# Hybrid attention layer on one core: taking GpSimd out of the projections

## The chip, the cores and the metric

The kernel runs on one core of a Trainium2 chip. The metric is the device time of one execution in microseconds. What is quoted is the median of several runs.

## What is computed

The reference is one decoder layer on 512 tokens of width 1024, all in float32:

```python
h = rms_norm(x, attn_pre_norm)
proj = h @ w_in                 # dq dk dv | nq | kc vc ks vs kw vw | gates
dq, dk, nq, kc, ks, kw = (apply_rope(t, cos, sin) for t in ...)
o_diff = diff_attention(dq, dk, dv, lam)       # 4 heads, two softmax maps each
o_nsa  = nsa_attention(nq, kc, vc, ks, vs, kw, vw, gates, ...)   # 8 heads, 3 branches
x = x + rms_norm(concat(o_diff, o_nsa) @ w_out, attn_post_norm)
h = rms_norm(x, ffn_pre_norm)
x = x + rms_norm((silu(h @ w_gate) * (h @ w_up)) @ w_down, ffn_post_norm)
```

`apply_rope` takes the halves x1, x2 of a head and returns x1·cos − x2·sin and x1·sin + x2·cos. The `nsa` branch also compresses kc and vc through a small two-layer network (`w1`, `w2`).

## The kernel before

**Precision.** TensorE multiplies rounded values (float32r). Each operand is therefore split into a rounded high part and a low part that holds the rest, and a product is the sum of three: high by high, high by low, low by high. For a weight tile of 128x1024 this is `split_w` (lines 108 to 113): a rounding copy `whi` (line 104 on ScalarE, 106 on VectorE) and a subtraction `wlo` (line 112, on VectorE or GpSimd). Raw weights, high and low parts have three buffers each, so a DMA for a new weight tile waits until a low part three tiles earlier is done.

**Start.** `load_x` brings the eight 128x512 pieces of the transposed x, and makes `xh` (line 195, ScalarE), `xl` (196, VectorE) and, in place over the raw piece, its square (199, GpSimd). VectorE adds the squares (203); TensorE sums them over the partitions, and from that come `rstd` and the four tables cos, sin, ckv, skv, which carry the factor rstd (line 246, in which VectorE reads the factor from PSUM).

**Projections.** The list `ORDER` writes the order of the stages. `C` is the pair kc, vc; `q0 k0 q1 k1 n0 n1 s` are the seven other pairs of 128x512 tiles (the two halves of the rotated heads); `v0 v1` and `g` are the projections that need no rotation; `ck cv` are the two compressions. One tile of a pair is `fm_tile`: 24 matmuls of 512 columns into one PSUM bank. These banks have the tag `mm`, of which there are two; `v`, `g`, the compressions and the later `mixp` use the same tag, and a compression holds its bank until its last weight tile has come. After each tile ScalarE copies PSUM to SBUF with the scale (line 282), and four products with the tables follow: t1, t2 (283, 284) on VectorE, a·sin, b·cos (285, 286) and then the sum (293), the second low part (300) and the odd tile's weight low part (112) on `e2`. `e2` is GpSimd for six of the eight pairs and VectorE for the two in `FAST`. The rotated high and low parts go to DRAM, and the heads load them from there.

**Who rounds.** `HIF`, `HIT` and `HIQ` name the weights (of pairs 1 and 5, of g, v0 and v1) and the rotated values (of pairs 1, 6 and 7) whose rounding VectorE does in place of ScalarE. `alt` gives every second low part of v0, g and the compressions to GpSimd.

**Heads and the rest.** `D0` to `D3` and `N0` to `N7` are attention heads. They are built with a higher priority, so that they are interleaved with the later projections from about 125 us on. In them GpSimd multiplies rows of the softmax (`row_mul`, line 505). After them come the output projection, the norms and the feed-forward products; these last run from about 354 us to the end.

**Order on the engines.** A planner orders the instructions of every engine before the run, from the priorities, the data they need and its own costs; on the chip each engine takes its list in that order. All DMAs are issued by the queue of SP, in order too.

Of the kernel before, what the change touches and what calls it, by code (L numbers as in the profile page):

```python
# [12 lines left out]
AF = mybir.ActivationFunctionType  # L13
OP = mybir.AluOpType
# [26 lines left out]
NVG = 4 * HEAD_DIM + 3 * NSA_HEADS  # L41
DQ0, DK0, KCVC, DQ1, DK1, NQ0, KSKW, NQ1 = range(8)
# [5 lines left out]
    "D3 F0 F1 M3 N7"  # L48
)
HP = 400  # L50
FAST = (1, 3)
POOL_LO = "157"
PSB = {"mm": 2, "sc": 3, "tr": 2, "av": 1}
MIX_A = (0, 1, 4, 5)
# [9 lines left out]
HP2 = 1  # L64
NS = 36
WB = (3, 3, 3)
LOD = ("v1",)
HP3 = 60
PREE = "adad"
TRH = ("tr", "gu", "tr", "tr")  # L70
HIF = (1, 5)
HIT = ("g", "v0", "v1")
HIQ = (1, 6, 7)
OTH = "a"
OTL = "p"
HIS = "d"
# [4 lines left out]
def hybrid_block_kernel(  # L81
# [6 lines left out]
    act, dve, pool, pe = nc.scalar, nc.vector, nc.gpsimd, nc.tensor  # L88

    def f32(ap):  # L90
        return ap.bitcast(F32)
# [10 lines left out]
    def to_r(eng, dst, src):  # L102
        if eng == "a":
            act.activation(dst, src, AF.Copy)  # L104
        else:
            dve.tensor_copy(dst, src)

    def split_w(raw, w=1024, lo_eng=None, hi_eng="a"):
        hi = wpool.tile([P, 1024], F32R, tag="hi", name="whi", bufs=WB[1])
        lo = wpool.tile([P, 1024], F32R, tag="lo", name="wlo", bufs=WB[2])  # L110
        to_r(hi_eng, hi[:, :w], raw[:, :w])
        (lo_eng or dve).tensor_tensor(lo[:, :w], raw[:, :w], f32(hi[:, :w]), OP.subtract)  # L112
        return hi, lo
# [42 lines left out]
    def sslot(name, dt=F32R):  # L156
        return S.tile([P, SEQ], dt, tag="s", name=name)
# [6 lines left out]
    def ps(tag, name, dt=F32):  # L164
        return PS.tile([P, SEQ], dt, tag=tag, name=name, bufs=PSB[tag])
# [18 lines left out]
    def rope_tile():  # L184
        return R.tile([P, 4, SEQ], F32R, tag="rope", name="rope")
# [3 lines left out]
    def load_x(k):  # L189
        if k % 2 == 0:  # L190
            xraws[k // 2] = T.tile([P, 2, SEQ], F32R, tag="k", name="xraw", bufs=BUFS["k"])
        t = f32(xraws[k // 2][:, k % 2])
        nc.sync.dma_start(t, xT[:, k])
        h, l = sslot(f"xh{k}"), sslot(f"xl{k}")
        act.activation(h, t, AF.Copy, scale=gc[:, k:k + 1])
        dve.scalar_tensor_tensor(l, t, gc[:, k:k + 1], f32(h), OP.mult, OP.subtract)  # L196
        xh.append(h)
        xl.append(l)
        pool.tensor_tensor(t, t, t, OP.mult)
        if sqs[k % 2] is None:  # L200
            sqs[k % 2] = t
        else:
            dve.tensor_tensor(sqs[k % 2], sqs[k % 2], t, OP.add)

    def load_fm(m):
        raws[m] = load_w(wf[m])
# [53 lines left out]
    def fm_tile(m, lo_eng=None):  # L260
        hi, lo = split_w(raws.pop(m), lo_eng=lo_eng, hi_eng="d" if m // 2 in HIF else "a")
        pt = ps("mm", f"fm{m}")
        seq = [(hi, xh), (hi, xl), (lo, xh)]
        n = 0
        for w, xx in seq:
            for k in range(NK):
                pe.matmul(pt, w[:, k * P:(k + 1) * P], xx[k], start=(n == 0), stop=(n == 3 * NK - 1))  # L267
                n += 1
        return pt

    def rope_pair(pair, scale, c=None, s=None):
        e2 = dve if pair in FAST else pool
        c = cos if c is None else c
        s = sin if s is None else s
        wide = rope_tile()
        t2, t1, b, a = (f32(wide[:, j]) for j in range(4))
        for o, half in ((a, 0), (b, 1)):
            m = 2 * pair + half
            if m not in raws:
                load_fm(m)  # L280
            pt = fm_tile(m, lo_eng=e2 if m % 2 else dve)
            act.activation(o, pt, AF.Copy, scale=scale)
        dve.tensor_tensor(t1, a, c, OP.mult)
        dve.tensor_tensor(t2, b, s, OP.mult)
        e2.tensor_tensor(a, a, s, OP.mult)
        e2.tensor_tensor(b, b, c, OP.mult)
        return wide, a, b, t1, t2

    def qk_pair(pair, scale):
        e2 = dve if pair in FAST else pool  # L290
        wide, a, b, t1, t2 = rope_pair(pair, scale)
        dve.tensor_tensor(t1, t1, t2, OP.subtract)
        e2.tensor_tensor(a, a, b, OP.add)
        d = dram.tile([4, HALF, 4, SEQ], F32, name=f"qk{pair}")
        hi1, lo1, hi2, lo2 = (wide[:, j] for j in range(4))
        hq = "d" if pair in HIQ else "a"
        to_r(hq, hi1, t1)
        to_r(hq, hi2, a)
        dve.tensor_tensor(lo1, t1, f32(hi1), OP.subtract)
        e2.tensor_tensor(lo2, a, f32(hi2), OP.subtract)  # L300
        nc.sync.dma_start(d.rearrange("m d c t -> (m d) c t"), f32(wide))
        return d

# [24 lines left out]
    def hie(tok):  # L328
        return "d" if tok in HIT else "a"

    def alt(tok, c):
        return pool if c % 2 and tok not in LOD else dve

    def dv_half(c2):
        ws, res = [], []
        for c in range(2):
            raw = load_w(wdv[c2][:, 1024 * c:1024 * (c + 1)])
            ws.append(split_w(raw, lo_eng=alt(f"v{c2}", c), hi_eng=hie(f"v{c2}")))
        for i in range(NT):
            pt = ps("mm", f"dv{i}")[:, :256]  # L340
            n = 0
            for k, xx, wi in [(k, xx, wi) for c in range(2) for xx, wi in ((xh, 0), (xl, 0), (xh, 1))
                              for k in range(4 * c, 4 * c + 4)]:
                w = ws[k // 4][wi][:, (k % 4) * 256:(k % 4 + 1) * 256]
                pe.matmul(pt, xx[k][:, i * P:(i + 1) * P], w, start=(n == 0), stop=(n == 3 * NK - 1))
                n += 1
            t = sslot(f"dv{i}")
            res.append(t)
            h, l = t[:, :256], t[:, 256:]
            act.activation(h, pt, AF.Copy, scale=rstd[:, i:i + 1])  # L350
            dve.scalar_tensor_tensor(l, pt, rstd[:, i:i + 1], f32(h), OP.mult, OP.subtract)
        return res

    def vg_proj():
        ws = []
        for c in range(3):
            nk = min(3, NK - 3 * c)
            raw = load_w(wvg[:, 3 * c:3 * c + nk].rearrange("p k n -> p (k n)"), nk * NVG)
            ws.append(split_w(raw, nk * NVG, lo_eng=alt("g", c), hi_eng=hie("g")))
        res = []  # L360
        for i in range(NT):
            pt = ps("mm", f"vg{i}")
            n = 0
            for k, xx, wi in [(k, xx, wi) for c in range(3) for xx, wi in ((xh, 0), (xl, 0), (xh, 1))
                              for k in range(3 * c, min(3 * c + 3, NK))]:
                w = ws[k // 3][wi][:, (k % 3) * NVG:(k % 3 + 1) * NVG]
                pe.matmul(pt[:, :NVG], xx[k][:, i * P:(i + 1) * P], w, start=(n == 0), stop=(n == 3 * NK - 1))  # L367
                n += 1
            vn = sslot(f"vn{i}").rearrange("p (b h d) -> p b h d", b=4, h=2)
            pv = pt[:, :4 * HEAD_DIM].rearrange("p (b d) -> p b d", b=4)  # L370
            act.activation(vn[:, :, 0], pv, AF.Copy, scale=rstd[:, i:i + 1])
            dve.scalar_tensor_tensor(vn[:, :, 1], pv, rstd[:, i:i + 1], f32(vn[:, :, 0]), OP.mult, OP.subtract)
            act.activation(gates[:, i], pt[:, 4 * HEAD_DIM:NVG], AF.Exp, scale=nrstd[:, i:i + 1])
            res.append(vn)
        dve.tensor_scalar_add(gates, gates, 1.0)
        dve.reciprocal(gates, gates)
        g0 = gates[:, 0].rearrange("p (h b) -> p h b", b=3)[:, :, 0]
        dve.tensor_scalar(g0, g0, valid, None, OP.mult)
        return res


    def compress(d, v, w1, w2, posd, w2cols):
# [30 lines left out]
                xs.append(hv)  # L413
        for c in range(4):
            raw = load_w(w1[:, 4 * c:4 * c + 4].rearrange("(a d) l n -> d a (l n)", d=HALF))
            hi, lo = split_w(raw, lo_eng=alt("cv" if v else "ck", c), hi_eng=hie("cv" if v else "ck"))
            for l in range(4):
                lh = 4 * c + l
                st = xs[lh // 4][:, lh % 4].rearrange("p s n -> p (s n)")
                for wi, w in enumerate((hi, lo)):  # L420
                    pe.matmul(hps[:2 * n2, :CMP_HIDDEN], st, w[:, l * 256:(l + 1) * 256],
                              start=(lh == 0 and wi == 0), stop=(lh == NLH - 1 and wi == 1))
        hs = tslot("chs", tag="c")
        act.activation(hs[:2 * n2, :CMP_HIDDEN], hps[:2 * n2, :CMP_HIDDEN], AF.Copy)
        pt = ps("tr", f"cht{v}")
# [357 lines left out]
    def halves(t):  # L783
        return [t[:, sl] for sl in CS]
# [108 lines left out]
    ws = [split_w(load_w(wd[f])) for f in range(NF - LAST, NF)]  # L893
    for i in range(NT):
# [3 lines left out]
        u, a, x_ = work("uf"), acc[i], halves(x2[i])  # L898
# [96 lines left out]
```

## Time and profile before

| | |
|---|---|
| median of 3 runs | 741.35 us (741.0 to 741.99) |
| the profiled execution: time, span of its instructions | 739.27 us, 737.4 us |
| TensorE matmuls, busy | 691.0 us (94%), 3536 instructions |
| VectorE busy | 505.9 us (69%), 790 |
| ScalarE busy | 290.3 us (39%), 621 |
| GpSimd busy | 161.8 us (22%), 128 |
| mean granted clock of TensorE | 0.971 |

A share is that of the whole span. GpSimd has work only in the first 360 us. A matmul's row lasts from its issue to its end, and the next one starts before that, so a busy TensorE is not one at its peak.

### The profile page before, as it was taken

The numbers are of one execution on the slowest core, as the hardware profiler recorded it, in microseconds if no ns is written. First come the engines' busy times: TensorE is split into PE (matmuls) and PEld (weight loads), VectorE is DVE, ScalarE is ACT, GpSimd is POOL, SyncE is SP. The second block draws the span as 40 slices with busy tenths as digits, with TensorE's granted clock in tenths as the row PEclk, the third lists the DMA queues.
The fourth block names the chain that finished last, engine by engine and source line by source line (L and its number), as shares of the span: only waits on it lengthen the run. The fifth ranks groups of instructions, "written<-read, shape, count | busy, mean of one in ns | idle before, by whom it ended". The sixth has DMA issues, their size and how long they took to land.

```text
span 737.4 us, 9477 instructions
## 1 busy us (share of the span) xinstructions
PE 691.0 (94%) x3536; PEld 569.9 (77%) x3536; DVE 505.9 (69%) x790; ACT 290.3 (39%) x621; POOL 161.8 (22%) x128
## 2 busy tenths in 40 slices
PE   7896989989999989998789999999999999999995
PEld 4785867879787877876788888888888888888884
DVE  6767898888899997568766776776766863212216
ACT  4224242335677986535522233233233232212113
POOL 5435445642455532205300000000000000000000
PEclk8999999999999999899799999999999999999998
DMA  9333848635132030163012322322232232232203
GB/s 316 109 127 116 285 159 272 244 140 186 59 100 86 16 116 1 57 204 140 29 42 76 112 86 86 103 97 87 91 109 85 87 109 91 86 106 94 88 26 115
DMA packets 25982, 83.64 MB, mean 113 GB/s; under 512 B 3408, under 2 KB 4304, under 8 KB 25040
## 3 DMA queue, kind: packets, MB, share of 16 engines
q1 hardware_dynamic: 25936, 83.03, 33.5%
q8 instruction: 28, 0.46, 0.3%
q14 instruction: 18, 0.15, 0.1%
HBM read 73.06 MB, written 9.96 MB: 113 GB/s over the span
## 4 chain that ended last, share of the span: by engine, by line
PE 70%; DVE 14%; ACT 4%; issue 2%; DMA 0%; POOL 0%; DVEq 0%; ACTq 0%
PE gu L845 34%; PE acc L884 15%; PE fm L267 4%; PE tr L496 2%; PE mixp L671 2%; PE avn L624 2%; PE vg L367 2%; PE sc L480 2%; DVE nm L484 2%; PE sc L481 1%; DVE p L540 1%; PE mix L683 1%; DVE wlo L112 1%; PE av L547 1%; ACT p L486 1%
## 5 line engine op out<-in xcount | busy, mean ns | idle before, releaser
L112 DVE TENSOR_TENSOR wlo<-wraw,whi 128x1024 fp32r<-128x1024 f32 (+1 forms) x84 | 105.8, 1259 | 136.9 <-ACT whi L104 89.0
L104 ACT ACTIVATE whi<-wraw 128x1024 fp32r<-128x1024 f32 x85 | 89.9, 1059 | 198.5 <-PE gu L845 92.5
L845 PE MATMUL gu<-hth,whi 128*128 128x512 f32 (+1 forms) x352 | 87.4, 391 | 0.0
L845 PE MATMUL gu<-htl,whi 128*128 128x512 f32 (+1 forms) x352 | 86.4, 385 | 0.0
L845 PE MATMUL gu<-hth,wlo 128*128 128x512 f32 (+1 forms) x352 | 85.5, 385 | 0.0
L845 PEld LDWEIGHTS gu<-hth,whi 128*128 128x128 f32 x352 | 65.6, 194 | 14.9 <-ACT hth L817 0.3
L845 PEld LDWEIGHTS gu<-htl,whi 128*128 128x128 f32 x352 | 64.4, 188 | 14.7
L845 PEld LDWEIGHTS gu<-hth,wlo 128*128 128x128 f32 x352 | 64.0, 187 | 14.7
L851 DVE RECIPROCAL silu<-silu 128x512 f32<-128x512 f32 (+1 forms) x24 | 74.1, 3086 | 0.8
L505 POOL TENSOR_TENSOR p<-p,l 128x384 f32<-128x384 f32 (+3 forms) x60 | 50.3, 866 | 68.4 <-DVE l L606 40.3
L486 ACT ACTIVATE p<-sc,nm 128x128 f32<-128x128 f32 (+1 forms) x96 | 50.3, 531 | 28.2 <-DVE nm L484 27.1
L884 PE MATMUL acc<-whi,ffl 128*128 128x512 f32 x144 | 56.0, 389 | 0.0
L884 PE MATMUL acc<-wlo,ffh 128*128 128x512 f32 x144 | 56.0, 389 | 0.0
L884 PE MATMUL acc<-whi,ffh 128*128 128x512 f32 x144 | 55.9, 389 | 0.0
L484 DVE TENSOR_REDUCE nm<-sc 128x1 f32<-128x128 f32 (+1 forms) x96 | 42.4, 480 | 7.2 <-PE sc L482 7.1
L267 PE MATMUL fm<-xh,whi 128*128 128x512 f32 x128 | 36.9, 429 | 3.0 <-ACT whi L104 2.2
L501 DVE TENSOR_TENSOR ptl<-tr,pth 128x384 fp32r<-128x384 f32 (+1 forms) x60 | 34.9, 592 | 5.8 <-ACT pth L500 5.5
L500 ACT ACTIVATE pth<-tr 128x384 fp32r<-128x384 f32 (+1 forms) x60 | 31.5, 528 | 17.5 <-PE tr L496 17.0
L112 POOL TENSOR_TENSOR wlo<-wraw,whi 128x1024 fp32r<-128x1024 f32 (+1 forms) x12 | 31.6, 2631 | 26.0 <-ACT whi L104 13.9
L496 PE MATMUL tr<-ident,p 128*128 128x128 f32 x200 | 33.3, 279 | 3.7 <-DVE p L540 2.3
L267 PE MATMUL fm<-xl,whi 128*128 128x512 f32 x128 | 33.9, 398 | 2.8 <-DVE xl L196 2.8
L480 PE MATMUL sc<-kst,qst 128*128 128x128 f32 (+2 forms) x96 | 35.3, 369 | 1.3 <-DVE pc L581 1.0
(232 smaller groups left out, 1317.5 us busy)
## 6 DMA issues: line engine op xcount, KB each, us to landing
wraw<-in_wg SPq DMA_DIRECT2D x22, 512.0 KB, 3.3
wraw<-in_wu SPq DMA_DIRECT2D x22, 512.0 KB, 3.3
wraw<-in_wd SPq DMA_DIRECT2D x22, 512.0 KB, 3.3
wraw<-in_wf SPq DMA_DIRECT2D x16, 512.0 KB, 3.8
qk<-rope SPq DMA_DIRECT2D x7, 1024.0 KB, 4.5
kst<-qk SPq DMA_DIRECT2D x24, 256.0 KB, 3.7
qst<-qk SPq DMA_DIRECT2D x16, 256.0 KB, 2.7
wraw<-in_wo SPq DMA_DIRECT2D x8, 512.0 KB, 4.1
```

The lines of the kernel that those rows point to most:

```text
L104: act.activation(dst, src, AF.Copy)
L112: (lo_eng or dve).tensor_tensor(lo[:, :w], raw[:, :w], f32(hi[:, :w]), OP.subtract)
L267: pe.matmul(pt, w[:, k * P:(k + 1) * P], xx[k], start=(n == 0), stop=(n == 3 * NK - 1))
L480: pe.matmul(sv, lhs, kk[:, 0, :w], start=True, stop=False)
L484: dve.tensor_reduce(nm, sv, AX.X, OP.max, negate=True)
L486: act.activation(pt, sv, AF.Exp, bias=nm, accum_out=l[:, i:i + 1])
L496: pe.transpose(tr[:, n * P:(n + 1) * P], pts[i][:, j * P:(j + 1) * P], ident)
L501: dve.tensor_tensor(ptl[:, sl], trv, f32(pth[:, sl]), OP.subtract)
L505: pool.tensor_tensor(p, p, l.to_broadcast(list(p.shape)), OP.mult)
L845: pe.matmul(pt, w_col(ww, k), hx[:, k, s0:s1], start=(n == 0), stop=(n == 3 * NK - 1))
L851: dve.reciprocal(sl, sl)
L884: pe.matmul(acc[i][c], a[f][:, i * P:(i + 1) * P], w[wi][:, c * SEQ:(c + 1) * SEQ], start=(first and n == 0), stop=(last and n == 2))
```

## The change

All GpSimd work of the projections goes to other engines. The squares of x go to ScalarE (line 199). All weight low parts go to VectorE, and all roundings to ScalarE. The four products of a rotation are made by VectorE straight from PSUM, with the scale inside the instruction, so that ScalarE's copy out of PSUM goes away; only the first pair (`C`), whose tables are not ready yet, is still copied raw to SBUF. The sum and the second low part go to VectorE in every pair. GpSimd keeps the row products in the heads, one memset in a compression, some low parts of `w_out` and of the head outputs, and multiplications in the norms.

```diff
-FAST = (1, 3)
-LOD = ("v1",)
-HIF = (1, 5)
-HIT = ("g", "v0", "v1")
-HIQ = (1, 6, 7)
+HIF = ()
+HIT = ()
+HIQ = ()
...
-        pool.tensor_tensor(t, t, t, OP.mult)
+        act.activation(t, t, AF.Square)
...
     def rope_pair(pair, scale, c=None, s=None):
-        e2 = dve if pair in FAST else pool
...
-        for o, half in ((a, 0), (b, 1)):
+        for half, outs in enumerate((((t1, c), (a, s)), ((t2, s), (b, c)))):
             m = 2 * pair + half
             if m not in raws:
                 load_fm(m)
-            pt = fm_tile(m, lo_eng=e2 if m % 2 else dve)
-            act.activation(o, pt, AF.Copy, scale=scale)
-        dve.tensor_tensor(t1, a, c, OP.mult)
-        dve.tensor_tensor(t2, b, s, OP.mult)
-        e2.tensor_tensor(a, a, s, OP.mult)
-        e2.tensor_tensor(b, b, c, OP.mult)
+            pt = fm_tile(m)
+            if pair == KCVC:
+                raw = f32(sslot("craw"))
+                act.activation(raw, pt, AF.Copy)
+                pt = raw
+            for o, tab in outs:
+                dve.scalar_tensor_tensor(o, pt, scale, tab, OP.mult, OP.mult)
         return wide, a, b, t1, t2
...
     def qk_pair(pair, scale):
-        e2 = dve if pair in FAST else pool
...
-        e2.tensor_tensor(a, a, b, OP.add)
+        dve.tensor_tensor(a, a, b, OP.add)
...
-        e2.tensor_tensor(lo2, a, f32(hi2), OP.subtract)
+        dve.tensor_tensor(lo2, a, f32(hi2), OP.subtract)
...
-    def alt(tok, c):
-        return pool if c % 2 and tok not in LOD else dve
...
-            ws.append(split_w(raw, lo_eng=alt(f"v{c2}", c), hi_eng=hie(f"v{c2}")))
+            ws.append(split_w(raw, hi_eng=hie(f"v{c2}")))
...
-            ws.append(split_w(raw, nk * NVG, lo_eng=alt("g", c), hi_eng=hie("g")))
+            ws.append(split_w(raw, nk * NVG, hi_eng=hie("g")))
...
-            hi, lo = split_w(raw, lo_eng=alt("cv" if v else "ck", c), hi_eng=hie("cv" if v else "ck"))
+            hi, lo = split_w(raw, hi_eng=hie("cv" if v else "ck"))
```

## Rows read from the trace of the kernel before

**Rows 1.** Windows of 100 us: busy time (instructions) per engine, clock, DMA share, GB/s.
```profile
0.00:100.00 100.00, 87.20 (x416) 69.46 (x416) 74.74 (x103) 34.27 (x56) 49.54 (x29) 0.93 0.55 190
100.00:200.00 100.00, 92.17 (x586) 79.56 (x585) 83.06 (x144) 45.07 (x121) 43.44 (x30) 1.00 0.51 178
200.00:300.00 100.00, 92.75 (x612) 75.43 (x611) 88.60 (x226) 76.02 (x226) 48.60 (x55) 0.96 0.20 61
```

**Rows 2.** Waits of TensorE, first 200 us: total, times, longest, in us.
```profile
PE cmp L421 <- DVE wlo L112: 5.2, 2, 4.3
PE fm L267 <- DVE xl L196: 2.8, 3, 1.6
PE tr L496 <- DVE p L540: 2.3, 2, 1.6
...
PE cmp L421 <- ACT whi L104: 1.6, 1, 1.6
...
PE kcp L439 <- DVE ce L436: 1.3, 1, 1.3
```

**Rows 3.** Timeline of TensorE, first 75 us: start, duration, in brackets idle before.
```profile
10.66 4.85 PE L267 MATMUL fm<-xh,whi 128*128 128x512 f32 x11 [0.69 <-ACT whi L104]
...
27.96 0.64 PE L345 MATMUL dv<-whi,xh 128*128 128x256 f32 x4
...
66.72 0.38 PE L421 MATMUL cmp<-whi,chl 128*124 128x256 f32 x1 [1.50 <-ACT rope L282]
...
73.43 0.57 PE L421 MATMUL cmp<-wlo,chl 128*124 128x256 f32 x1 [4.32 <-DVE wlo L112]
```

**Rows 4.** Chain of waits, first 200 us: one whole tile of 24 matmuls.
```profile
131.61 5.55 PE fm L267 x24
```

**Rows 5.** Timeline of VectorE, 65 to 120 us.
```profile
66.70 1.69 DVE L283 TENSOR_TENSOR rope<-rope,cos 128x512 f32<-128x512 f32 x1 [2.32 <-ACT rope L282]
...
70.01 3.37 DVE L112 TENSOR_TENSOR wlo<-wraw,whi 128x1024 fp32r<-128x1024 f32 x1
...
95.69 3.79 DVE L405 TENSOR_TENSOR cst<-cx,pos 128x248 f32<-128x248 f32 x2 [0.60 <-ACT w L394]
...
101.25 1.17 DVE L405 TENSOR_TENSOR cst<-cx,pos 128x248 f32<-128x248 f32 x2
...
118.27 2.42 DVE L432 TENSOR_SCALAR ce<-ce 128x124 f32<-128x124 f32 x1
```

**Rows 6.** Timeline of GpSimd, the same stretch.
```profile
69.50 2.79 POOL L112 TENSOR_TENSOR wlo<-wraw,whi 128x1024 fp32r<-128x1024 f32 x1
...
96.42 2.64 POOL L112 TENSOR_TENSOR wlo<-wraw,whi 128x1024 fp32r<-128x1024 f32 x1
...
117.98 2.62 POOL L112 TENSOR_TENSOR wlo<-wraw,whi 128x1024 fp32r<-128x1024 f32 x1 [4.62 <-DVE whi L106]
```

**Rows 7.** Line of `xl`, VectorE, first 200 us: durations min/median/max in ns, starts.
```profile
L196 DVE SCALAR_TENSOR_TENSOR xl<-xraw,gc,xh x8: 734/1128/2862, 5.4 to 21.5; 128x512 fp32r<-128x512 f32 x8
```

**Rows 8.** The same for VectorE's weight low parts.
```profile
L112 DVE TENSOR_TENSOR wlo<-wraw,whi x20: 1020/1220/3366, 7.3 to 186.5; 128x1024 fp32r<-128x1024 f32 x18, 128x840 fp32r<-128x840 f32 x1, 128x560 fp32r<-128x560 f32 x1
```

**Rows 9.** Groups by shape, VectorE, first 200 us: busy us, mean ns | idle before.
```profile
L106 DVE CAST whi<-wraw 128x1024 fp32r<-128x1024 f32 x8 | 6.6, 820 | 2.5 <-DMA wraw<-in_wf 2.5
...
L293 DVE TENSOR_TENSOR rope<-rope 128x512 f32<-128x512 f32 x2 | 1.4, 681 | 0.0
...
L246 DVE TENSOR_TENSOR ckv<-rb,ckv 128x512 f32<-128x512 f32 x1 | 0.7, 681 | 0.0
```

**Rows 10.** Groups by shape, ScalarE, first 200 us.
```profile
L104 ACT ACTIVATE whi<-wraw 128x1024 fp32r<-128x1024 f32 x21 | 22.0, 1054 | 21.9 <-DMA wraw<-in_wf 11.3 <-DMA wraw<-in_kw 3.7 <-PE fm L267 3.4
L282 ACT ACTIVATE rope<-fm 128x512 f32<-128x512 f32 x16 | 9.4, 589 | 17.7 <-PE fm L267 17.0 <-DVE wlo L112 0.7
...
L104 ACT ACTIVATE rope<-rope 128x512 fp32r<-128x512 f32 x8 | 5.0, 631 | 13.5 <-DVE rope L292 9.1 <-POOL rope L293 4.4
```

**Rows 11.** Group by shape, GpSimd, first 200 us.
```profile
L112 POOL TENSOR_TENSOR wlo<-wraw,whi 128x1024 fp32r<-128x1024 f32 x11 | 29.5, 2682 | 18.5 <-ACT whi L104 13.9 <-DVE whi L106 4.6
```

## The prediction

> **What bounds the kernel now.** I read the windows first, since the change lies almost wholly in the first 200 us. There TensorE is busy 87.20 and 92.17 of each 100 us [rows 1], so at most 20.6 us of its idle time can come back in this stretch, besides matmuls that are issued slowly inside "busy". VectorE is the next one: 157.8 of 200 us. ScalarE has 79.3 us and is mostly free; GpSimd has 93.0.
>
> Second, the waits of TensorE [rows 2]. The longest are on weight low parts (5.2 us, nearly all in one wait of 4.3), on `xl` at the start (2.8), on a softmax row of the first head (2.3), on a weight rounding of a compression (1.6) and on the compression's activation (1.3). All but the rounding end with VectorE.
>
> Third, why VectorE is late: its timeline beside that of GpSimd. A weight low part takes 1.22 us in the median and 3.37 at most [rows 8], and that longest one started 0.5 us after a GpSimd low part of 2.79 us [rows 5, 6]: counted from the end of the GpSimd instruction at 72.29 it ran 1.09 us, about its ordinary time. The two additions of a compression took 3.79 us beside a GpSimd low part that ended at 99.06, and the same two 1.17 without one. A scalar operation on 124 columns took 2.42 us and ended 0.09 us after another. `xl` takes 0.73 at best and 2.86 at worst [rows 7]. So a VectorE instruction that meets a GpSimd one stands for the rest of it, and the four longest waits of TensorE are downstream of such meetings.
>
> **The start.** TensorE needs two tiles of 24 matmuls, 48 in all. Fifteen are issued by 15.36 us (four at 7.34 and eleven in the row at 10.66); the other 33 last until the next stage begins at 27.96, which is 12.6 us [rows 3]. At the rate of a whole tile, 24 in 5.55 us or 231 ns each [rows 4], 33 take 7.6 us. What holds them is `xl`, whose last starts at 21.5 [rows 7], because the squares and one low part run on GpSimd. Afterwards eight `xl` at 0.73, two low parts at 1.22 and six additions at the 0.68 of a 512-column VectorE operation [rows 9] are 12.4 us from about 7 us on, so even with the additions in front they end by 20, and the `xl` alone by 15. ScalarE's eight squares cost 0.63 each, as its 512-column roundings [rows 10]: 5.0 us in a stretch where it has little else. The DMAs are the same. Of the 5.0 us between 12.6 and 7.6 I take 4.5.
>
> **The compression of v, at 66 to 74 us.** Two waits of TensorE, 1.50 and 4.32 us [rows 3]. The low part loses 2.15 us of its 3.37, and the product ahead of it 1.0 of its 1.69 [rows 5, 9]; the one between them is as long. That is 4.1 us late by contention alone, and I take 4.1. The rest is a wait for the PSUM bank (below). **The compression of k.** TensorE's 1.6 us for a rounding, with a shorter wait for the low part behind it, follow from the additions that took 2.6 us too long [rows 2, 5]: 2.0. **Its activation:** 1.3 us, behind the operation of 2.42 us: 1.3. **The first head:** 2.3 us, where GpSimd's row products stay and only its rotation goes: 1.0. Sum of the gains: 4.5 + 4.1 + 2.0 + 1.3 + 1.0 = 12.9 us.
>
> **What VectorE takes on.** Twelve weight low parts at 1.22 (14.6 us), twelve rotation products, five sums and five second low parts at 0.68 (15.0 us): 29.6. It gives up eleven weight roundings, at most 0.82 each [rows 9], and six roundings of rotated values, under 0.68 each as half-size casts: some 10 us by what they take undisturbed. Net +20 us, and the meetings shown above alone give back 2.15 + 1.0 + 2.6 + 2.2 and, by the median of `xl`, at least 3.3: 11 us. So its 42 us of idle time in this stretch shrinks by 9 at most. Cost on the path: 0, because that idle time covers it; without cover, 9 us, the upper bound.
>
> **Products from PSUM.** The trace has no scalar-tensor-tensor with 512 columns of PSUM. The nearest is the table product at line 246, one operand in PSUM, 681 ns, against 681 ns for the sum at line 293 with both in SBUF [rows 9]. I take 0.68 for each. [...]
>
> **The PSUM bank.** ScalarE's copy of 0.59 us freed the bank [rows 10]; now two products in VectorE's queue do, 1.3 us or so, 0.7 later for each of 14 tiles. Two banks exist and the next tile fills the other for 5.55 us, which hides it, except while a compression holds one. TensorE's wait of 1.50 us at 66.72 is of that kind already. Lower bound 0; upper bound 14 tiles times 0.7 plus one queued low part of 1.22, 27 us. I take three uncovered tiles, 2.0 us, near the lower end, because only the two compressions take the cover away.
>
> **What ScalarE takes on.** Eight squares and six rotated roundings at 0.63, eleven weight roundings at up to 1.05, less fourteen copies at 0.59 [rows 10]: 8.8 + 11.6 − 8.2 = 12 us on an engine with 120 us idle here. A rounding takes 0.4 us longer than VectorE's undisturbed one; three weight buffers hide it. Taken as 0; bounds 0 and 11 times 0.4, 4 us. The squares overwrite what `xl` reads, so each waits for its `xl`; queued behind a waiting square would be the next `xh` and weight roundings, and TensorE behind them. Within the start's bound, 0 to 4.5.
>
> **Queues.** No DMA is added. SP's queue holds the weight loads behind the low parts that free their buffers, and with those 1.4 us shorter than GpSimd's 2.68 [rows 8, 11] loads leave earlier. I count nothing for it. No instruction is moved past POOL's queue.
>
> **After 200 us** the heads run on, VectorE busy 88.60 of 100 [rows 1]. Nothing there is edited. I take it that they begin and end earlier by what the projections gain.
>
> Net: 12.9 − 2.0 = 10.9 us. The profiled execution took 739.27 us, 1.9 more than its span of 737.4, so 728.4; the median shown, 741.35, is 2.1 above it, and against that I forecast **730.4 us**.
>
> **Rivals.** *The heads take the gain back* (small gain or none). VectorE's 83 of the second 100 us holds head work as well as projections. If VectorE is the limit there and not TensorE, the work from GpSimd after 125 us delays the heads: three low parts, four products, three sums and three second low parts, 3.7 + 6.8 = 10.5 us, less five roundings (about 3.5): 7 us of the 10.9, so 737. For it speaks VectorE's 88.60 right after; against it, 17 us of idle time in that stretch and the meetings that end.
>
> *VectorE as the only one to free banks* (slower). TensorE waits after most tiles, since the products stand behind weight low parts and softmax maxima in VectorE's fixed order. It decides from 12.9 / 14 = 0.9 us of wait for each tile; at 2 us it costs 28, which gives 741.35 − 12.9 + 28 = 756. For it: VectorE is 79% busy, and a compression, `v` and `g` share the two banks. Against it: 5.55 us of cover for each tile outside them.
>
> *All waits go* (more): TensorE idle only where data has not come. Nearly all of the 20.6 us, so about 721.
>
> *The contention stays*: GpSimd still has the heads' row products, and VectorE still meets those. It touches only the 1.0 of the first head, so it is no case of its own.
>
> **How the numbers follow.** A measurement of this kernel can tell about 0.2%, 1.5 us, from no change. The sum's own case, a gain of 6 to 16 us (725.3 to 735.3): 0.52. More than 16: 0.11. Small gain, 1.5 to 6, by the first rival: 0.13. Within 1.5: 0.06. Slower, by banks or by an order of the planner that loses elsewhere: 0.18. Faster is 0.52 + 0.11 + 0.13 = 0.76. For 8 in 10 I leave out what lies beyond the third rival's 721 with some slack for issue time inside "busy" (below 718, 0.04) and the part of the second rival above 744 (0.13).
>
> **What would show it.** Right: `xl` at 0.73 throughout, the first `dv` matmul near 23.5 instead of 27.96, no low part near 3 us before 125, the 4.32 us wait gone, `dv` and `vg` ended 10 us earlier, and VectorE busy about 150 to 167 of the first 200 us. Wrong: TensorE waits on the new products that add up to more than 2 us, ScalarE's squares ahead of `xh` at the start, or heads that start earlier and end at the same time. The prediction falls if TensorE's idle time in the first 200 us is not below 14 us.

## The result, and the profile after

The median went from 741.67 us (741.0 to 742.29) to **719.16 us** (717.87 to 720.81), 4 runs of each; the ratio is 0.970, its 95% interval 0.968 to 0.973. That is 22 us faster, where 730.4 was forecast. The profiled execution took 718.04 us with a span of 716.3, so 21.1 us of span are to be accounted for. Line numbers of the changed kernel are 2 to 6 lower: `wlo` is at line 110, `xl` at 194, a tile's matmuls at 265, and the new products from PSUM at 284.

The busy times on the page of the changed kernel:
```profile
PE 684.8 (96%) x3536; PEld 566.4 (79%) x3536; DVE 491.0 (69%) x807; ACT 300.0 (42%) x632; POOL 79.7 (11%) x86
```
The windows that answer to [rows 1]:
```profile
0.00:100.00 100.00, 91.99 (x465) 75.60 (x466) 75.61 (x129) 46.95 (x72) 0.73 (x5) 0.95 0.63 210
100.00:200.00 100.00, 97.02 (x625) 82.68 (x624) 81.66 (x172) 53.71 (x150) 22.33 (x25) 1.00 0.50 174
200.00:300.00 100.00, 95.54 (x620) 79.48 (x621) 82.75 (x206) 74.28 (x210) 40.09 (x45) 0.97 0.21 64
```
TensorE's idle time in the first 200 us fell from 20.6 to 8.01 + 2.98 = 11.0 us. VectorE is busy for 157.3 of them, as against 157.8 before, but the kernel has got further by then. Up to the last matmul of the projections (the last `vg`, below) VectorE was busy for 149.8 us before and is for 131.9 now, though it does the low parts, products and sums that GpSimd had.

TensorE's waits in the first 200 us, as in [rows 2]; all those of 0.5 us and more but the one at the warm-up:
```profile
PE fm L265 <- ACT whi L102: 2.9, 2, 2.2
PE fm L265 <- DVE chl L406: 2.1, 1, 2.1
...
PE sc L474 <- DVE pc L575: 1.2, 1, 1.2
PE tr L490 <- DVE ptl L495: 0.9, 3, 0.6
PE dv L339 <- DVE dv L345: 0.7, 1, 0.7
PE cmp L415 <- DVE wlo L110: 0.5, 1, 0.5
```
The waits for `xl` and for `ce` are gone, and that for low parts went from 5.2 to 0.5. The first line, a rounding on ScalarE, lies at the very start (7.77 and 11.60 us) and had its like there before, in a line that [rows 2] leaves out:
```profile
PE fm L267 <- ACT whi L104: 2.2, 2, 1.6
```
The second line, 2.1, names `chl`, which the waiting matmul doesn't read. The timelines of TensorE, ScalarE and VectorE:
```profile
92.66 0.79 PE L265 MATMUL fm<-xh,whi 128*128 128x512 f32 x2 [2.07 <-DVE chl L406]
```
```profile
90.62 1.99 ACT L102 ACTIVATE whi<-wraw 128x1024 fp32r<-128x1024 f32 x2
```
```profile
90.48 0.69 DVE L284 SCALAR_TENSOR_TENSOR rope<-fm,cos 128x512 f32<-128x512 f32 x1
```
The product of line 284, the last reader of a PSUM bank while a compression held the other, ended at 91.17, and the two roundings at 92.61, just ahead of the matmul. So far as these ends tell, TensorE waited some 0.6 us for the bank and then some 1.4 for a rounding.

The lines of `xl` and of the weight low parts, as in [rows 7] and [rows 8]:
```profile
L194 DVE SCALAR_TENSOR_TENSOR xl<-xraw,gc,xh x8: 741/745/751, 5.6 to 17.4; 128x512 fp32r<-128x512 f32 x8
...
L110 DVE TENSOR_TENSOR wlo<-wraw,whi x32: 732/1220/1247, 7.8 to 169.5; 128x1024 fp32r<-128x1024 f32 x29, 128x840 fp32r<-128x840 f32 x2, 128x560 fp32r<-128x560 f32 x1
```
The medians of the low parts are equal; only the tail, 3366 ns before and 1247 now, has gone. The groups of the new products, VectorE, first 150 us:
```profile
L284 DVE SCALAR_TENSOR_TENSOR rope<-fm,cos 128x512 f32<-128x512 f32 x14 | 9.6, 686 | 2.9 <-PE fm L265 2.8
L284 DVE SCALAR_TENSOR_TENSOR rope<-fm,sin 128x512 f32<-128x512 f32 x14 | 9.6, 686 | 4.1 <-PE fm L265 4.1
```
A product from PSUM takes 686 ns, and but for those 0.6 us it is VectorE that waits for TensorE ahead of it, not the reverse.

**Where the 21.1 us came from.** Starts of some TensorE matmuls, from the tile views of both traces and of four experiments below, in us:

| first or last of | before | after | earlier by | a_read | a_write | a_sbufrope | a_rows |
|---|---|---|---|---|---|---|---|
| `dv`, first | 28.0 | 25.1 | 2.9 | 24.6 | 24.7 | 25.6 | 25.4 |
| `cmp`, first | 66.7 | 60.4 | 6.3 | 65.2 | 59.9 | 59.9 | 60.6 |
| `cmp`, last | 111.0 | 99.7 | 11.3 | 110.6 | 99.7 | 99.2 | 98.1 |
| `vg`, last (projections end) | 191.7 | 174.0 | 17.7 | 189.2 | 173.9 | 169.2 | 168.2 |
| `sc`, last (scores of the heads) | 291.8 | 274.1 | 17.7 | 289.4 | 274.0 | 282.1 | 283.1 |
| `gu`, first (feed-forward) | 354.5 | 337.6 | 16.9 | 354.2 | 337.4 | 344.8 | 340.5 |
| `gu`, last | 609.8 | 588.6 | 21.2 | 605.6 | 588.7 | 594.2 | 592.3 |

Two cautions for reading it. Single executions of one order scatter: a_write has the order of the changed kernel on the four engines and lies within 0.5 us of it in every row; b_hp2 (below) has that of the kernel before up to 339 us, and yet its last `cmp` comes 1.6 us later and its last `sc` 2.2. And the last `vg` is not the same point of the work in all of them: in a_sbufrope, a_rows, a_nopool, b_lows and b_rounds the planner put 27 matmuls of the heads behind it (12 `av`, 9 `scc`, 6 `sc`; some 3.5 us by their mean times) that stand ahead of it in the changed kernel, and the kernel before has six `sc` more ahead of it, 0.8 us.

So 17.7 us come out of the projections, the heads and the output projection return 0.8, and 4.2 come later, from code that the change doesn't touch. The second row of the projections, as a window of before (the first is in [rows 1]) and of after:
```profile
100.00:191.70 91.70, 84.12 (x530) 72.97 (x529) 75.07 (x120) 38.68 (x100) 38.84 (x24) 1.00 0.56 194
```
```profile
100.00:174.00 74.00, 73.93 (x476) 65.05 (x475) 56.30 (x106) 35.38 (x92) 5.27 (x6) 1.00 0.61 212
```
With the first 100 us, TensorE's idle time up to the last `vg` was 12.80 + 7.58 = 20.4 us and is now 8.01 + 0.07 = 8.1: 12.3 us less. The other 5.4 lie inside "busy": 945 matmuls took 171.3 us, now 939 take 165.9. A part of this is the clock. Windows of TensorE in the kernel before, with the granted clock after the busy time:
```profile
22.00:25.30 3.30, 3.01 (x7) 0.50 0.00 0
25.40:70.00 44.60, 41.70 (x245) 1.00 0.33 107
73.20:76.50 3.30, 3.07 (x11) 0.50 0.59 197
```
In the first stretch at 0.50 a matmul of a tile, at 22.29, took 0.80 us, where the median of those is 0.39. That stretch follows waits for `xl` of 0.79 and 1.61 us, the one from 73.2 the wait of 4.32 for a low part. In the first lies a run of eight low-part products, at 22.89, that took 3.16 us and takes 1.98 now, at 19.59. The changed kernel has one such stretch, at 93.3 to 96.5 with 0.50, behind its wait of 2.07; and both kernels have one of some 7 us at the start, also with 0.50. In all of them together, up to the last `vg`, TensorE was busy for 12.3 us before and is for 9.2 now. An estimate, with half of that time as the cost, as 0.80 us beside 0.39 suggests: 1.5 of the 5.4 us are the clock. The six `sc` are another 0.8. The remaining 3.1 are matmuls that were issued late inside their rows, not told apart further.

### The profile page after: what moved, and what is told of

Its sections match the earlier page's. It is cut to its first block, busy times and chain, and to the rows that moved or that the text cites. A ratio compares the mean times of both kernels' runs of the same rounds, so it can differ in the third digit from the quotient of the medians.

```text
span 716.3 us, 9446 instructions
## 1 busy us (share of the span) xinstructions
PE 684.8 (96%) x3536; PEld 566.4 (79%) x3536; DVE 491.0 (69%) x807; ACT 300.0 (42%) x632; POOL 79.7 (11%) x86
## 4 chain that ended last, share of the span: by engine, by line
PE 79%; DVE 13%; ACT 3%; DMA 2%; issue 1%; SPq 0%; DVEq 0%; ACTq 0%
PE gu L839 35%; PE acc L878 15%; PE fm L265 10%; PE tr L490 2%; PE mixp L665 2%; PE avn L618 2%; PE dv L339 2%; PE vg L361 2%; DVE nm L478 2%; PE sc L474 2%; DMA wraw<-in_wf 2%; PE sc L475 1%; PE mix L677 1%; PE av L541 1%; DVE rope L284 1%
## 5 line engine op out<-in xcount | busy, mean ns | idle before, releaser
L110 DVE TENSOR_TENSOR wlo<-wraw,whi 128x1024 fp32r<-128x1024 f32 (+2 forms) x96 | 116.5, 1216 | 140.5 <-ACT whi L102 92.2
L102 ACT ACTIVATE whi<-wraw 128x1024 fp32r<-128x1024 f32 (+2 forms) x96 | 100.7, 1051 | 212.6 <-PE gu L839 88.5
L265 PEld LDWEIGHTS fm<-xh,whi 128*128 128x128 f32 x128 | 25.6, 205 | 13.1 <-ACT whi L102 6.2
```

## Experiments

Theory A is the prediction's: a VectorE instruction that meets one of GpSimd stands for the rest of it, and what ended was that. In its narrow form only instructions with two operands in SBUF stand, and only beside GpSimd's reads. Theory B is the rival that the chain of a rotation got shorter, without a copy on ScalarE and slow products on GpSimd, and that contention matters little. All ratios are to the kernel before, run on the same chip. Those kernels whose names begin with a_ start from the changed kernel, those with b_ from the kernel before.

**GpSimd's reads given back, and nothing else (a_read, a_write, a_read3).** After every rotation GpSimd does work of its own on a private 128x512 tile, which nobody reads, 48 instructions in all. Nothing is left out, and the order of the other engines' instructions is that of the changed kernel.
```diff
...
+    def busy(src):
+        pool.tensor_copy(junkp[:, :1], src[:, :1])
+        for _ in range(6):
+            pool.tensor_tensor(junkp, junkp, junkp, OP.mult)
...
             for o, tab in outs:
                 dve.scalar_tensor_tensor(o, pt, scale, tab, OP.mult, OP.mult)
+        busy(t1)
```


> The changed kernel with GpSimd made busy again by work that nobody needs: after the products of each of the eight rotations it multiplies a private 128x512 tile by itself six times, 48 instructions that read and write SBUF. PE, VectorE, ScalarE and SP keep exactly the order they have in the changed kernel, and nobody waits for the private tile. Theory A (VectorE loses time when it meets a GpSimd instruction that reads SBUF, and TensorE waits for VectorE): 4 to 12 us slower than the changed kernel, so 723 to 731 us, with weight low parts of 2 us and more in the first 150 us. Theory B (the gain comes from the new order and the shorter rotation chain, not from the meetings): within 1.5 us of the changed kernel, 718 to 721.

Measured: 736.02 us, ratio 0.993 (0.991 to 0.996). Private reads on an otherwise idle engine cost 17 of the 22 us, more than A expected. The dose is not that of the kernel before (GpSimd is busy for 72.4 us up to the last `vg`, 88.4 there), so the 17 are no measure of each term; but with it the first `gu` comes at 354.2, as against 354.5 before, and what is left of the gain is the 4 us of the feed-forward. Groups of VectorE in a_read, first 150 us:
```profile
L110 DVE TENSOR_TENSOR wlo<-wraw,whi 128x1024 fp32r<-128x1024 f32 x28 | 42.2, 1517 | 7.4 <-ACT whi L102 6.5 <-issue 0.6 <-ACT l L253 0.3
L292 DVE SCALAR_TENSOR_TENSOR rope<-fm,cos 128x512 f32<-128x512 f32 x14 | 9.5, 681 | 0.2 <-PE fm L273 0.2
...
L298 DVE TENSOR_TENSOR rope<-rope 128x512 f32<-128x512 f32 x7 | 7.2, 1026 | 0.0
```
Low parts took 1517 ns instead of 1223 and the rotation's subtraction 1026 instead of 680, both with two inputs in SBUF; the product with one input in PSUM took 681 ns, as against 686. It can be seen in single instructions. GpSimd's timeline in a_read, and VectorE's over it:
```profile
62.04 9.01 POOL L264 TENSOR_TENSOR junkp<-junkp 128x512 f32<-128x512 f32 x6
```
```profile
62.16 2.00 DVE L110 TENSOR_TENSOR wlo<-wraw,whi 128x1024 fp32r<-128x1024 f32 x1
64.09 1.52 DVE L306 TENSOR_TENSOR rope<-rope 128x512 fp32r<-128x512 f32 x1
65.53 0.68 DVE L292 SCALAR_TENSOR_TENSOR rope<-fm,sin 128x512 f32<-128x512 f32 x1
...
70.08 1.53 DVE L299 TENSOR_TENSOR rope<-rope 128x512 f32<-128x512 f32 x1
71.53 1.21 DVE L110 TENSOR_TENSOR wlo<-wraw,whi 128x1024 fp32r<-128x1024 f32 x1
```
VectorE's windows up to the last `vg`, in a_read and in the changed kernel, the same 235 instructions in the same order:
```profile
0.00:189.20 189.20, 157.39 (x235) 0.95 0.57 194
```
```profile
0.00:174.00 174.00, 131.91 (x235) 0.97 0.62 211
```
VectorE's busy time rose by 25.5 us, and the last `vg` came 15.2 later: each microsecond on VectorE cost 0.6 on the path. Of the 15.2, 11.5 are idle time of TensorE and 3.7 lie inside "busy". There the clock stood at 0.50 for longer, with 16.0 us of busy time as against 9.2; by the estimate above that is 3.4 of the 3.7. So 11.5 us of waits came, by that estimate, with 3.4 more for the clock behind them.

a_write has `pool.memset(junkp, 0.0)` in place of the multiplication.

> The same as the run before, but the 48 private instructions are memsets, which write SBUF and read nothing; order on the other engines unchanged. Theory A in its narrow form (VectorE's second SBUF input meets GpSimd's reads): within 2 us of the changed kernel, 718 to 721, and weight low parts stay near 1.22 us. Theory A in its wide form (any GpSimd work at the same time): as the run with reads, in proportion to the shorter busy time, 3 us or more. Theory B: no change.

Measured: 719.24 us, ratio 0.971 (0.967 to 0.975), the changed kernel's time. The group of these writes, GpSimd, and that of the low parts, VectorE, in a_write:
```profile
L264 POOL MEMSET junkp<- 128x512 f32 x48 | 25.6, 533 | 2.8
```
```profile
L110 DVE TENSOR_TENSOR wlo<-wraw,whi 128x1024 fp32r<-128x1024 f32 x28 | 34.0, 1221 | 8.3 <-ACT whi L102 7.9 <-ACT l L253 0.3
```
The 48 writes cost TensorE nothing here, 719.24 us as against 719.16: the loss of 17 us in a_read is not GpSimd being busy, and not its instructions or waits, but goes with the multiplications, which read SBUF where the memsets don't. In the mean a low part took 1517 ns in the run with the multiplications and 1221 in that with the memsets, and the product from PSUM 681 and 686.

VectorE's busy time up to the last `vg` rose by 1.0 us, to 132.9, and that is four instructions with a single input, in SBUF, which met a memset and took 0.27 to 0.28 us longer each (two `CAST`, two `TENSOR_SCALAR`). One of them, 0.43 us in the changed kernel:
```profile
117.35 0.70 DVE L104 CAST ws<-wraw 128x512 fp32r<-128x512 f32 x1
```
So the narrow form holds for most of what cost time, and is a little too narrow for VectorE as a whole.

a_read3 has three multiplications after each rotation, 24 in all.

> The changed kernel with half the private reading work: three multiplications after each rotation, 24 in all, other engines in the same order. With 48 it was 17 us slower than with memsets. Theory A: 6 to 11 us slower than the changed kernel (725 to 730). A threshold (small doses are hidden by TensorE's own work): under 4 us.

Measured: 726.1 us, ratio 0.982 (0.979 to 0.985). That is what A expected. a_write stands for no reads. The three runs come from two chips, so their ratios are compared, 0.971, 0.982 and 0.993 for 0, 24 and 48 reads: the first 24 cost 7.9 us of 741 and the next 24 8.5, alike within the intervals, 0.33 to 0.36 us each. No point at which slack takes it up was found. The 24 reads kept GpSimd busy for 32.8 us (1368 ns each); the 48 writes kept it busy for 25.6 and cost nothing, so the shorter time of the writes is not what spares them.

**The parts of the change, each alone on the kernel before.**
```diff
# b_lows: all weight low parts to VectorE
-            pt = fm_tile(m, lo_eng=e2 if m % 2 else dve)
+            pt = fm_tile(m)
...
-        return pool if c % 2 and tok not in LOD else dve
+        return dve
# b_rope: products from PSUM, sums and second low parts on VectorE
...
+                dve.scalar_tensor_tensor(o, pt, scale, tab, OP.mult, OP.mult)
...
-        e2.tensor_tensor(a, a, b, OP.add)
+        dve.tensor_tensor(a, a, b, OP.add)
...
# b_squares: squares on ScalarE
-        pool.tensor_tensor(t, t, t, OP.mult)
+        act.activation(t, t, AF.Square)
# b_rounds: all roundings on ScalarE
-HIF = (1, 5)
+HIF = ()
...
-HIQ = (1, 6, 7)
+HIQ = ()
```


> The kernel before with one part of the change: all twelve weight low parts that GpSimd made go to VectorE; rotations, squares and roundings stay as they were. Theory A: 4 to 9 us faster than before (733 to 738), since 31.6 of GpSimd's 84 us in the projections go away, the longest meetings among them. Theory B (the shorter rotation chain and the start give the gain): less than 2 us either way.

> The kernel before with another part alone: the rotation products from PSUM on VectorE, its sums and second low parts on VectorE; weight low parts, squares and roundings stay as they were. Theory A: 4 to 9 us faster than before (733 to 738), as 36 us of GpSimd work go. Theory B: 10 us or more faster, since this is the part that shortens the chain from PSUM to DRAM. If VectorE frees the PSUM banks too late: slower.

> The kernel before with the squares of x on ScalarE and nothing else. Theory A, by the prediction's term for the start: 3 to 5 us faster (736 to 738 against a before of 741), the first dv matmul 3 to 5 us earlier. Rival (the start is set by the DMAs and by ScalarE's queue): within 1.5 us, or slower where a square stands ahead of an xh.

> The kernel before with all roundings of the projections on ScalarE, GpSimd's work unchanged. Theory A: small, -2 to +2 us: VectorE gets some 10 us of its time back and a few meetings fewer, but each rounding takes 0.4 us longer. Rival (VectorE's load is what counts, not the meetings): 3 us faster or more.

Measured, against 0.970 for the whole:

| | median, us | ratio (95%) | projections end earlier by | first to last `gu`, us |
|---|---|---|---|---|
| b_lows | 727.42 | 0.982 (0.978 to 0.986) | 16.9 | 249.4 |
| b_rope | 731.51 | 0.987 (0.983 to 0.991) | 4.4 | 251.6 |
| b_squares | 737.89 | 0.996 (0.994 to 0.997) | 2.3 | 255.1 |
| b_rounds | 740.02 | 0.999 (0.998 to 1.001) | 6.4 | 250.3 |

The kernel before has 255.3 in the last column. Low parts carry most, and gained more than A expected. But of b_lows' 12.4 us of span 5.9 came in the feed-forward, and of b_rope's 6.9, 3.7; by the first `gu` they were ahead by 6.4 and 3.2. b_rope's gain as a whole lies on the border between what A and B expected and so separates nothing. b_squares gained some 3 us by its ratio, at A's lower edge, but not as A said: its first `dv` came at 28.0, as before. There `xl` took 734 to 753 ns, as A expected, but TensorE waited 1.8 us for `xh`, which ScalarE made behind squares, as the rival said, and the sums of the squares came ahead of `dv`. Roundings alone give no gain, as A expected. The four shares add up to 3.6% where the whole has 3.0: the feed-forward's step is in three of them. The last two columns say why a single ratio tells little here: b_rounds ended its projections 6.4 us earlier (in b_lows and b_rounds some 4 us of this are head matmuls that moved behind them) and the feed-forward took 5.0 less, yet its first `gu` came 6.1 later than before, at 360.6, so the stretch between took it all.

**Is it the product from PSUM? (a_sbufrope)** The rotation goes back to ScalarE's copies, with all four products on VectorE from SBUF.
```diff
...
-            for o, tab in outs:
-                dve.scalar_tensor_tensor(o, pt, scale, tab, OP.mult, OP.mult)
+            act.activation(o, pt, AF.Copy, scale=scale)
+        dve.tensor_tensor(t1, a, c, OP.mult)
+        dve.tensor_tensor(t2, b, s, OP.mult)
+        dve.tensor_tensor(a, a, s, OP.mult)
+        dve.tensor_tensor(b, b, c, OP.mult)
```


> The changed kernel with the rotation as it was: ScalarE copies each tile to SBUF with the scale and VectorE makes the four products from there; GpSimd stays out of the projections. It separates reading PSUM from leaving GpSimd. Theory A: within 3 us of the changed kernel (717 to 722), since no GpSimd instruction comes back. Theory B (the shorter chain from PSUM): 5 us or more slower. [...]

Measured: 725.0 us, ratio 0.979 (0.977 to 0.980), 6 us slower than the changed kernel; A's expectation missed, and B's number was met. But the projections ended at 169.2, 4.8 us *earlier* than with products from PSUM. Some 3.5 of these are the 27 matmuls that moved behind them, and TensorE's idle time up to there is 8.0 us, as against 8.1: so it isn't the rotation that loses, nor does it win much. The loss is in the heads, where TensorE now waits for the softmax; its longest waits from 169.2 to 282.1 us:
```profile
PE scc L565 <- ACT p L479: 3.9, 5, 1.4
PE trc L589 <- DVE ptl L494: 3.0, 2, 2.8
```
In the changed kernel the first of these is 1.2 us in two, and the second is not among its waits.

**Do the roundings on ScalarE pay inside the whole? (a_rounds)** The three tuples go back.
```diff
-HIF = ()
-HIT = ()
-HIQ = ()
+HIF = (1, 5)
+HIT = ("g", "v0", "v1")
+HIQ = (1, 6, 7)
```


> The changed kernel with the roundings of pairs 1 and 5, of g, v0 and v1, and of the rotated pairs 1, 6 and 7 back on VectorE. Theory A: 0 to 3 us slower than the changed kernel (719 to 722), as VectorE carries 10 us more and ScalarE has idle time. Rival (ScalarE's queue is now what the weights wait for): faster than the changed kernel.

Measured: 725.07 us, ratio 0.979 (0.977 to 0.981), 6 us slower than the whole. Only 1.5 of it was lost by the last `vg` and 2.5 by the first `gu`; 3.5 came in the feed-forward, which took 254.5 us instead of 251.0. Ahead of that A's 0 to 3 holds.

**The feed-forward, which nobody edited (b_hp2).** First to last `gu` takes 255.3, 255.1 and 254.5 us in the kernel before, b_squares and a_rounds, and 249.4 to 251.8 in the eleven others. In the three the planner put the last norm's `rs` behind a second reciprocal of the feed-forward. VectorE's timeline, and then TensorE's, in the kernel before:
```profile
368.67 1.75 DVE L851 RECIPROCAL silu<-silu 128x256 f32<-128x256 f32 x1
370.34 0.10 DVE L130 TENSOR_TENSOR rs<-rr 128x1 f32<-128x1 f32 x1
```
```profile
371.90 1.29 PE L814 MATMUL trh<-ident,mixt 128*128 128x128 f32 x8 [2.62 <-DVE mixt L809]
```
The same in the changed kernel:
```profile
350.48 0.16 DVE L128 TENSOR_TENSOR rs<-rr 128x1 f32<-128x1 f32 x1
...
353.02 1.75 DVE L845 RECIPROCAL silu<-silu 128x256 f32<-128x256 f32 x1
```
```profile
352.25 1.29 PE L808 MATMUL trh<-ident,mixt 128*128 128x128 f32 x8 [0.16 <-DVE mixt L803]
```
Behind its wait the kernel before ran at a granted clock of 0.50 once more, where the changed kernel and b_hp2 have 1.00. Window of TensorE, before:
```profile
373.60:376.90 3.30, 3.30 (x17) 0.50 0.02 5
```
The wait is 2.46 us longer than in the changed kernel, and half of that stretch is 1.7: by this estimate the two are the 4.2. b_squares and a_rounds have the same wait, of 2.63 and 2.62 us, and the same stretch behind it: their longest `gu` matmuls of `hth` by `whi` took 582 and 580 ns, 584 in the kernel before, and 416 in the changed kernel.

b_hp2 is the kernel before with only the priority of those norms raised, which puts `rs` ahead; up to the norms its order on TensorE is unchanged.
```diff
-HP2 = 1
+HP2 = 5
```


> The kernel before with one number changed, HP2 = 5 for 1, the priority step of the norms after the attention. All engines keep the order of the kernel before until those norms; there VectorE makes the last norm's factor ahead of the second reciprocal of the first feed-forward tiles, as in the changed kernel. Theory C (some 4 us of the 21 come from this flip in the planner's order, not from the projections): 3 to 5 us faster than before, and from the first to the last feed-forward matmul some 251 us instead of 255. Rival (that stretch is faster because GpSimd and VectorE meet less in it): no change.

Measured: 737.13 us, ratio 0.997 (0.994 to 0.999). The stretch took 251.1 us, 4.2 less, with TensorE's wait at the same place down to 0.15 us. The step of 4.2 is thus shown to come from the planner's order, and to be had without the change. The whole gained less than expected, 2.6 us by the ratio: in the profiled execution the first `gu` came 2.9 later. Of these, 2.2 stand already at the last `sc`, ahead of the first instruction that changed its place, so they are scatter and no price of the order.

**The rest of GpSimd's reads (a_rows, a_nopool).** If reads cost so much, the heads' row products should go to VectorE too, and in a_nopool also the low parts of `w_out` and of the head outputs.
```diff
-NSC = "appp"
-DSC = "pdpp"
+NSC = "addd"
+DSC = "dddd"
# a_nopool as well:
-POOL_LO = "157"
-OTL = "p"
+POOL_LO = ""
+OTL = "d"
```


> The changed kernel with the row products of the heads on VectorE, where GpSimd had three of four: GpSimd keeps only some low parts and the norms. Theory A carried on: VectorE takes some 60 products of 0.2 to 0.4 us, 15 us, and loses the meetings; 3 to 8 us faster than the changed kernel (711 to 716). Rival (in the heads VectorE's load sets the end, and its second operand mostly comes from PSUM there, so that it meets GpSimd seldom): 3 us slower or more.

> The run before, and the low parts of w_out and of the head outputs on VectorE too, so that GpSimd does nothing between the start and the norms. Theory A: 0 to 4 us faster than the run before. Rival: slower than it by the 9 subtractions that VectorE takes on, up to 6 us.

Measured: 721.37 us, ratio 0.975 (0.972 to 0.979), and 724.25, 0.979 (0.974 to 0.983). Neither beats the changed kernel, so the theory carried on to the heads fell. With a_rows the projections ended at 168.2, 5.8 us earlier still (some 3.5 of it the 27 matmuls), and the heads 9 later. VectorE is nearly as full as TensorE there, 102.7 and 104.3 of 114.9 us, and 60 of the 64 row products took it 395 to 479 ns where 0.2 to 0.4 us was expected; TensorE's longest wait became the softmax:
```profile
PE sc L474 <- ACT p L480: 4.9, 8, 1.2
```
In the heads the long low parts (`ptl`) subtract out of PSUM and took the same time, 681 and 682 ns in the mean, for 512 columns with GpSimd's products beside them and without: there was less to win.

No version that was run beats the changed kernel.

## Why the prediction came out as it did

The mechanism was right and is shown: meetings of VectorE with GpSimd's reads held TensorE, and giving such reads back with everything else in place takes 17 us of the gain. The size was off: the gain lies above the 6 to 16 us of the sum's own case, and a gain above 16 had a chance of 0.11. In its reading of the waits the prediction passed over one, the 2.2 us for a rounding at the start, which is still there. By the prediction's own steps:

- **The start, 4.5.** The first two tiles ended at 28.13 us before and end at 23.61 now: 4.5. Of these only 1.9 are idle time; 2.6 lie inside "busy", with the stretch at a clock of 0.50 from 22.0 to 25.3, which the sum didn't name. Timeline of TensorE after:
```profile
21.62 1.99 PE L265 MATMUL fm<-xh,wlo 128*128 128x512 f32 x8
23.45 1.84 PE L235 MATMUL ssum<-ones,xraw 128*128 128x1 f32 x16
25.15 0.72 PE L339 MATMUL dv<-whi,xh 128*128 128x256 f32 x4
```
  The first `dv` still came at 25.15 and not 23.5, since the 16 sums of the squares, spread over the later `dv` before, now stand ahead of it. That is work moved, not lost: by the first `cmp` the lead is 6.3 us.
- **The compressions, 4.1 + 2.0, less 2.0 for the bank: 4.1 net.** From the first to the last `cmp` the lead grew by 5.0. Of the bank's 2.0 there came some 0.6 us, in the wait of 2.07 beside a compression; three tiles uncovered was too many.
- **The activation and the first head, 1.3 + 1.0.** Mis-sized most. Between the last `cmp` and the last `vg` the lead grew by 6.4 us: TensorE's idle time from 111.0 to 191.7 us fell from 1.33 + 3.43 to 0.07 from 99.7 to 174.0. The 1.33 is the activation's wait, sized rightly. Of the other 3.43 (2.3 of it the softmax row named in the prediction) the sum took 1.0, since GpSimd's row products stay. They do: of GpSimd's 24 instructions from 100 us to the last `vg` before, 38.84 us, six are row products, and six row products, 5.27 us, are all that is left there now. But the other 18 went, and the waits went whole. How much of that is the order was not tried alone: between the long scores and the first transposes of that head TensorE now has 30 matmuls of `dv`, which the planner put there, and had 8. With the same order and the reads of a_read the stretch takes 78.6 us, as against 74.3 now and 80.7 before.
- **"The sum of the gains"** was made of waits alone. The idle time that ended is 12.3 us, close to the 12.9 of the sum, but in part by luck: the start has less of it than its term and the first head more. What the sum lacked is most of the 5.4 us inside "busy", the clock of 0.50 behind the waits among them: the prediction named slow issue at the outset, but gave it room in the range only, and doesn't name the clock.
- **VectorE's added load, 0.** Right: 157.3 us, inside 150 to 167, though with more of the heads in it. Up to the last `vg` VectorE's busy time fell from 149.8 to 131.9. Since by the prediction's count some 20 us were taken on net, some 38 must have been given back by meetings that ended, not the 11 counted; this is worked out, not measured. **Products from PSUM at 0.68:** 0.686, beside 680 and 689 ns for the subtraction and the sum from SBUF in the same kernel.
- **ScalarE, 0.** Not quite: TensorE's wait for a rounding at the start grew from 2.2 to 2.9 us, and some 1.4 of the wait of 2.07 are for one, so 2.1 together, inside the bounds of 0 and 4. Taking the roundings back lost 1.5 us by the end of the projections all the same, which is within the scatter of single executions.
- **"After 200 us ... nothing there is edited"**, and the lead is passed on. It was, but for 0.8 us, through the heads. The step failed in the feed-forward: 4.2 us came from an order of the planner that flipped some 175 us behind the last edited instruction, which for the size of the gain is luck. The prediction counted such flips only as a way to lose.

Together: 12.3 + 5.4 − 0.8 + 4.2 = 21.1 us of span, against 10.9 forecast. Of the rivals, "all waits go" (721) is nearest in time but not in kind: 11.0 us of idle time are left in the first 200. There are no bank waits but the 0.6 us, and no heads that take the gain back. (In a_read, with VectorE slowed, TensorE did wait for a product from PSUM, 2.6 us in one.)

**Open:** why a_sbufrope and a_rows, with projections that end 5 to 6 us earlier, have their last scores 8 to 9 us later. Some 3.5 us are the 27 matmuls that moved, and the clock granted in that stretch was 0.94 and 0.96 as against 1.00 in the changed kernel. The waits for the softmax show the place; whether the planner's order or the load on ScalarE and VectorE makes them was not tried. The heads' reaction also limits what each part's ratio says of that part.

## What to carry to other kernels

Where VectorE and GpSimd share a stretch, look at the tail of equal VectorE instructions, not at the mean: here the longest low part took 3.37 us against a median of 1.22, beside a GpSimd one of 2.79, and VectorE with that GpSimd work moved onto it was busy for 131.9 us up to the last `vg` instead of 149.8. Price such meetings by more than the waits that they cause by name: matmuls issued late inside a busy row and stretches at a clock of 0.50 behind the waits came on top here, some 4.6 us to 12.3. Compare busy times over the same work, not over windows of the same length: over 200 us VectorE seemed as busy as before, over the projections it was busy 17.9 us less. And with a planner, split the gain by stages before believing it, and see that a stage holds the same instructions: in three of fourteen kernels here a far stage was some 4 us longer, in one of them shown to be for its order alone, and in five 27 matmuls had crossed the end of a stage.

## What the runs showed of the hardware

- Beside GpSimd's 128x512 multiplications a VectorE subtraction of 1024 columns with two inputs in SBUF took 2.00 us instead of 1.21, one of 512 columns 1.52 instead of 0.69. In the run with 48 memsets the former took 1221 ns in the mean, as against 1223 without them.
- Some instructions with a single input in SBUF took longer too: two `CAST`s of 512 columns 1262 ns in the mean in a_read, as against 422 in the changed kernel, and one 0.70 us beside a memset in a_write, instead of 0.43.
- GpSimd's 48 multiplications in a_read took 1039 ns at best, 1125 in the median, 1336 in the mean and 1905 at most; what made the longer ones was not shown.
- TensorE's granted clock in the kernel before was 0.50 in stretches behind its waits: from 73.2 to 76.5 us behind one of 4.32, and from 373.6 to 376.9 behind one of 2.62, with 1.00 between 25.4 and 70.0.
- A product of 512 columns with one operand in PSUM took 681 and 680 ns in the mean in a_read and 686 in the changed kernel; there a subtraction and a sum of 512 columns with both operands in SBUF took 680 and 689.
